# The first feed-forward's up projection as seven block products instead of eight

## The chip, the cores and the metric

The kernel runs on one core of a Trainium2 chip. Its time is the device time of that core in microseconds (us), from one launch; the time before is the median of three runs. The core has TensorE (PE; its weight loads are a row of their own, PEld), VectorE (DVE), ScalarE (ACT), GpSimd (POOL) and SyncE (SP), which issues most of the DMAs. Each engine works through its own queue of instructions in order; semaphores tie the queues together.

## The reference

A two-layer transformer on 512 latent tokens and 256 context tokens, model width 1024. Each layer has a mixer (attention in layer 0, a gated recurrence, HGRN2, in layer 1) and a feed-forward; before each of them comes a norm whose shift and scale come from conditioning vectors (the adaptive norm).

```python
def rms_norm(x, w):
    y = x * lax.rsqrt(jnp.mean(x * x, axis=-1, keepdims=True) + NORM_EPS)
    return y * w
def modulate(h, shift, scale):
    return h * (1.0 + scale) + shift
def swiglu(h, w_in, w_out):
    a, u = jnp.split(h @ w_in, 2, axis=-1)       # w_in is 1024 x 5632, a and u have 2816 columns
    return (jax.nn.silu(a) * u) @ w_out          # w_out is 2816 x 1024

for i in range(2):
    mod_l = silu(c) @ ada_w[i] + ada_b[i]        # 6 chunks of 1024; the same with c_ctx for the context
    ...
    h = h + gt1_l * y_l                          # the mixer
    h = h + gt2_l * swiglu(modulate(rms_norm(h, norm_ffn_w[i]), sh2_l, sc2_l), ffn_w_in[i], ffn_w_out[i])
    if not last:                                 # layer 0 alone: the context tokens too
        hc = hc + gt1_c * y_c
        hc = hc + gt2_c * swiglu(modulate(rms_norm(hc, norm_ffn_w[i]), sh2_c, sc2_c), ffn_w_in[i], ffn_w_out[i])
return rms_norm(h, final_norm_w)
```

So the first feed-forward runs on T = 768 tokens, the second on 512. In both, the hidden width 2816 is 22 tiles of 128, and the contraction over 1024 is 8 k-steps of 128.

## The kernel before

Activations lie transposed: the tile `hT[k]` holds 128 channels on its partitions and 768 tokens on its columns. Every fp32 product is made of three matmuls of a reduced format, in `mm3` (L104 to L107): each operand is split into a part hi, a cast on ACT (L82), and the rest lo, a subtraction on DVE or POOL (L85); then hi·hi (L105), hi·lo (L106) and lo·hi (L107) are summed in PSUM. Weights come through a ring: `load_split` loads a raw tile of 128 x 1024 floats (512 KB, four buffers) by a DMA on SP's queue and splits it into `whi` and `wlo` (three buffers each).

A feed-forward, `ffn`, goes over the hidden tiles in three parts of 8, 7 and 7 (`PARTS`). For each hidden tile, `chain` makes the gate half and then the up half: 8 k-steps, on the spans 0:512 and 512:770, three matmuls each. The spans hold the 768 tokens and two more columns, the shift of the two kinds of token, since the operands `fnh` and `fnl` (L780, L781) are the residual times the scale, without the norm and the shift. The norm's factor `rst`, one per token, is multiplied in behind the matmuls (`scaled`, L835 to L838), where the bias column is added too: silu on ACT (L861), the product on DVE (L865), and the split of the hidden tile into `gh` and `gl`. At the end of a part its 7 or 8 hidden tiles go through the down projection (`fo_chain`), whose result is added onto the residual (`residual`, L646).

The token factors come from `token_scale`: squares on ACT, their sums on DVE and POOL (L238), then `rstd_cols` (a matmul with ones, L245, a power on POOL, L250) and `rstd_psum` (a diagonal per 128 tokens on DVE, L258, times ones on PE, L259). They are made under the first two hidden tiles' matmuls. At the end of the first feed-forward, `norm_tail` does the same for layer 1.

The last output projection of attention (`wo_gen` with g = 3, PSUM tiles `wo` and `wos`) closes the attention's own filler queue, on the spans of 512 and 256 tokens.

Between hidden tiles and down-projection tiles, `fill.step` lets a side job take a few steps: the sums of the adaptive norm, `ada_acc`. Each step multiplies a 128 x 1024 piece of `ada_w` (`adw`) by a scalar and adds it (L220, L222), on DVE. In the first feed-forward it makes chunk 5 of layer 0, the gate of this feed-forward's own residual, and behind part 0 (`ada_last`) six chunks of layer 1. Chunk 4 of layer 0 is made on PE during attention (`ada_chunk`, 32-column matmuls, `pa`).

The program is written as one sequence; a scheduler puts each instruction in its engine's queue and sets semaphores, and pools of buffers set how far ahead a load may go.

Of the kernel before, what the change touches and what calls it, by code (L numbers as in the profile page):

```python
# [16 lines left out]
P = 128  # L17
# [13 lines left out]
PARTS = [(0, 8), (8, 7), (15, 7)]  # L31
# [12 lines left out]
def kernel(  # L44
# [11 lines left out]
    dma = nc.sync.dma_start  # L56

# [46 lines left out]
    def mm3(ps, ahi, alo, bhi, blo, first, last):  # L104
        PE.matmul(ps, ahi, bhi, start=first, stop=False)  # L105
        PE.matmul(ps, ahi, blo, start=False, stop=False)  # L106
        PE.matmul(ps, alo, bhi, start=False, stop=last)  # L107
# [85 lines left out]
    def ada_reduce(layer, ch, accs, load, fp):  # L193
        nv = len(accs)
        part = fp.tile([P, 2, 32], F32, tag="adpart", name=f"adpart{layer}{ch}")
        for v, a in enumerate(accs):
            turned = load(f"adt{layer}{ch}{v}")
            DVE.transpose(turned, a)
            DVE.tensor_reduce(part[:, v], turned.rearrange("p (j r) -> p j r", r=32), op=ALU.add, axis=AX.X)
            yield  # L200
        yield
# [9 lines left out]
    folds = []  # L211

    def ada_acc(layer, ch, accs, load, fp):
        for k in range(KT):
            raw = load(f"adw{layer}{ch}{k}")
            dma(raw, ada_w[layer, k * P : (k + 1) * P, ch * D : (ch + 1) * D])
            for v, a in enumerate(accs):
                cc = csil[:, v, k : k + 1]
                if k == 0:
                    DVE.tensor_scalar(a, raw, cc, None, op0=ALU.mult)  # L220
                else:
                    DVE.scalar_tensor_tensor(a, raw, cc, a, op0=ALU.mult, op1=ALU.add)  # L222
                yield
        yield from ada_reduce(layer, ch, accs, load, fp)

# [5 lines left out]
    def sumsq_add(acc, sqp, h, k, first, eng=None):  # L231
        if first:
            ACT.activation(acc, h, AF.Square)
        else:
            sq = sqp.tile([P, T], F32, tag="sq", bufs=2, name=f"sq{k}")
            sq = sq[:, : h.shape[1]]
            ACT.activation(sq, h, AF.Square)
            (eng or DVE).tensor_tensor(acc, acc, sq, op=ALU.add)  # L238

    def rstd_cols(pl, accs, n):  # L240
        nt = n // P
        pc = bank("ssq")
        for t in range(nt):
            for i, acc in enumerate(accs):
                PE.matmul(pc[:, 2 * t : 2 * t + 2], acc[:, t * P : (t + 1) * P], ones[:, 0:2],  # L245
                          start=(i == 0), stop=(i == len(accs) - 1))
# [1042 lines left out]
```

## Time and profile before

| what | us |
|---|---|
| runs (three) | 1898.82, 1902.82, 1902.89; median 1902.82 |
| profiled execution: its time | 1901.45 |
| profiled execution: span from first to last instruction | 1899.4 |
| front: projections, start of attention | 0 to 233 |
| attention | 233 to 438.95 |
| first feed-forward (768 tokens) | 438.95 to 1016.4 |
| HGRN2 | 1016.4 to 1510 |
| second feed-forward and output | 1510 to 1899.4 |

The bounds of the stages are those at which the first matmul of a stage's tiles starts. The mean granted clock of TensorE over the span was 0.988 of full speed. Rows of the page name a line of the code, an engine, an operation, the tile written, an arrow, the tiles read, the shape and the count; then the busy time, the mean duration of one in ns, and the idle time of the engine just before, with what released it. A row of the timeline starts with the start time and the duration, and ends, in brackets, with how long the engine had waited and for what. A matmul's duration there overlaps the next one's, since they are pipelined.

### The profile page before, as it was taken

The numbers are of one execution on the slowest core, as the hardware profiler recorded it, in microseconds if no ns is written. First come the engines' busy times: TensorE is split into PE (matmuls) and PEld (weight loads), VectorE is DVE, ScalarE is ACT, GpSimd is POOL, SyncE is SP. The second block draws the span as 40 slices with busy tenths as digits, with TensorE's granted clock in tenths as the row PEclk, the third lists the DMA queues.
The fourth block names the chain that finished last, engine by engine and source line by source line (L and its number), as shares of the span: only waits on it lengthen the run. The fifth ranks groups of instructions, "written<-read, shape, count | busy, mean of one in ns | idle before, by whom it ended". The sixth has DMA issues, their size and how long they took to land. (4 is left out here: it accounts for less than half of the span.)

```text
span 1899.4 us, 29674 instructions
## 1 busy us (share of the span) xinstructions
PE 1833.4 (97%) x12111; PEld 1633.3 (86%) x12111; DVE 1127.6 (59%) x1821; ACT 680.3 (36%) x1222; POOL 394.8 (21%) x401
## 2 busy tenths in 40 slices
PE   8989999998999999999998989999998999999998
PEld 6778788887888888888887979889897799898997
DVE  3676788888866446445545555564647744344444
ACT  3333877763321122112224423233333432222224
POOL 1243534532000000000002444354436100000000
PEclk9989999998999999999999999999999999999999
DMA  9433200012424235353321211111111133333331
GB/s 325 169 104 100 100 2 23 23 46 78 155 89 133 79 93 174 88 154 107 100 66 51 79 45 45 57 56 56 56 56 45 45 93 97 89 89 98 92 88 57
DMA packets 206152, 166.37 MB, mean 88 GB/s; under 512 B 6801, under 2 KB 189249, under 8 KB 206017
## 3 DMA queue, kind: packets, MB, share of 16 engines
q1 hardware_dynamic: 205728, 163.43, 28.1%
q8 instruction: 96, 1.57, 0.3%
q10 hardware_dynamic: 288, 1.05, 0.1%
q14 instruction: 40, 0.32, 0.1%
HBM read 162.36 MB, written 2.10 MB: 87 GB/s over the span
## 5 line engine op out<-in xcount | busy, mean ns | idle before, releaser
L106 PE MATMUL ffi<-fnl,whi_fi 128*128 128x258 f32 (+2 forms) x1408 | 439.5, 312 | 2.6 <-DVE fnl L781 2.6
L105 PE MATMUL ffi<-fnh,whi_fi 128*128 128x258 f32 (+2 forms) x1408 | 440.3, 313 | 1.4 <-ACT fnh L780 1.3
L107 PE MATMUL ffi<-fnh,wlo_fi 128*128 128x258 f32 (+2 forms) x1408 | 437.5, 311 | 0.0
L106 PEld LDWEIGHTS ffi<-fnl,whi_fi 128*128 128x128 f32 x1408 | 268.2, 190 | 19.3 <-DVE fnl L781 3.6
L105 PEld LDWEIGHTS ffi<-fnh,whi_fi 128*128 128x128 f32 x1408 | 266.8, 190 | 18.0 <-ACT fnh L780 1.5
L107 PEld LDWEIGHTS ffi<-fnh,wlo_fi 128*128 128x128 f32 x1408 | 267.2, 190 | 15.9
L82 ACT CAST whi_fi<-raw_fi 128x1024 fp32r<-128x1024 f32 x88 | 92.3, 1050 | 359.0 <-issue 190.3
L250 POOL TENSOR_TENSOR rc<-rc,mhalf 128x2 f32<-128x2 f32 (+2 forms) x6 | 6.4, 1068 | 929.0 <-DVE rc L248 929.0
L105 PE MATMUL ffo<-gh,whi_fo 128*128 128x512 f32 (+1 forms) x542 | 192.2, 355 | 0.9 <-DVE modc L206 0.5
L107 PE MATMUL ffo<-gh,wlo_fo 128*128 128x512 f32 (+1 forms) x542 | 190.8, 352 | 0.0
L106 PE MATMUL ffo<-gl,whi_fo 128*128 128x512 f32 (+1 forms) x542 | 190.7, 352 | 0.0
L646 DVE SCALAR_TENSOR_TENSOR hT<-ffo,modc,hT 128x512 f32<-128x512 f32 (+1 forms) x74 | 47.8, 648 | 128.7 <-PE ffo L107 128.6
L222 DVE SCALAR_TENSOR_TENSOR adacc<-adw,csil,adacc 128x1024 f32<-128x1024 f32 x70 | 88.3, 1280 | 57.5 <-DMA adw<-in_ada_w_dram 57.3
L82 ACT CAST whi_fo<-raw_fo 128x896 fp32r<-128x896 f32 (+1 forms) x48 | 47.0, 980 | 202.5 <-PE ffo L106 98.5
L105 PEld LDWEIGHTS ffo<-gh,whi_fo 128*128 128x128 f32 x542 | 101.9, 188 | 16.8 <-issue 1.5
L106 PEld LDWEIGHTS ffo<-gl,whi_fo 128*128 128x128 f32 x542 | 101.9, 188 | 15.4
L107 PEld LDWEIGHTS ffo<-gh,wlo_fo 128*128 128x128 f32 x542 | 101.8, 188 | 15.3
L1103 POOL TENSOR_TENSOR KD<-KD,tot 128x384 f32<-128x384 f32 x96 | 100.3, 1068 | 68.7 <-ACT kc L1086 67.1
L85 DVE TENSOR_TENSOR wlo_fi<-raw_fi,whi_fi 128x1024 fp32r<-128x1024 f32 x87 | 106.1, 1221 | 7.5 <-ACT whi_fi L82 6.5
L660 POOL TENSOR_SCALAR pf<-pf,st 128x768 f32<-128x768 f32 (+1 forms) x96 | 73.7, 769 | 119.3 <-DVE st L659 75.5
L85 DVE TENSOR_TENSOR ptl<-pt,pth 128x384 fp32r<-128x384 f32 (+1 forms) x160 | 79.5, 522 | 9.7 <-ACT pth L82 8.4
L1103 DVE TENSOR_TENSOR QD<-QD,tot 128x256 f32<-128x256 f32 x96 | 56.3, 626 | 42.2 <-PE lv L1096 42.0
(315 smaller groups left out, 4203.2 us busy)
## 6 DMA issues: line engine op xcount, KB each, us to landing
raw_fi<-in_ffn_w_in_dram SPq DMA_DIRECT2D x88, 512.0 KB, 3.8
adw<-in_ada_w_dram SPq DMA_DIRECT2D x80, 512.0 KB, 4.3
raw_fo<-in_ffn_w_out_dram SPq DMA_DIRECT2D x32, 448.0 KB, 3.6
raw_fo<-in_ffn_w_out_dram SPq DMA_DIRECT2D x16, 512.0 KB, 3.8
raw_hz<-in_hgrn_w_in_dram SPq DMA_DIRECT2D x14, 512.0 KB, 3.8
adr<-in_ada_w_dram SPq DMA_DIRECT2D x16, 256.0 KB, 4.5
adr<-in_ada_w_dram SPq DMA_DIRECT2D x8, 512.0 KB, 7.0
raw_wq<-in_attn_w_qkv_dram SPq DMA_DIRECT2D x8, 512.0 KB, 5.5
```

The costliest lines, as they stand in the source:

```text
L82: ACT.copy(hi, src)
L85: (eng or DVE).tensor_tensor(lo, src, hi.bitcast(F32), op=ALU.subtract)
L105: PE.matmul(ps, ahi, bhi, start=first, stop=False)
L106: PE.matmul(ps, ahi, blo, start=False, stop=False)
L107: PE.matmul(ps, alo, bhi, start=False, stop=last)
L222: DVE.scalar_tensor_tensor(a, raw, cc, a, op0=ALU.mult, op1=ALU.add)
L250: POOL.tensor_tensor(rc, rc, mhalf.to_broadcast([P, nt]), op=ALU.pow)
L646: DVE.scalar_tensor_tensor(hT[o][:, a:e], ps, mcol(layer, ch, o, v), hT[o][:, a:e], op0=ALU.mult, op1=ALU.add)
L660: POOL.tensor_scalar(pf, pf, st3[:, 2:3], 1.0, op0=ALU.mult, op1=ALU.mult)
L1103: eng.tensor_tensor(view, view, f, op=ALU.mult)
```

## The change

In the first feed-forward the up projection, seen as a product of a matrix of weight blocks and a matrix of activation blocks, two by two each, is made by Strassen's scheme, in seven block products instead of eight. For one pair (the gate and the up half of one hidden tile) the four weight blocks are a11 and a12 (gate, k-steps 0 to 3 and 4 to 7) and a21 and a22 (up, the same); the four activation blocks are b11, b12 (k-steps 0 to 3, first and second half of the 768 tokens) and b21, b22 (k-steps 4 to 7). Each block product is four k-steps of three matmuls with 384 columns. The products m1 to m7 of a pair run in the order m1, m5, m2, m6, m4, m3, m7. Their results are put together partly in PSUM, where m6 and m7 add onto m1's bank and m3 onto m5's, and partly by copies and subtractions in SBUF (c11, c12, c21, c22).

- **Weight sums.** Four of the seven products need a sum or a difference of weight blocks. They are made in the raw tile of the ring, by DMAs on POOL's queue that add to their destination (`gather`, L834): a21 += a22 when the tile is loaded (S1), a21 += a11 after the split for m5 (S2), then a11 += a21 as it lies in HBM (S3), and a21 += a12 after the split for m6 (S4). Splits are now 512 wide, two to a ring tile, and `split_ahead` keeps three ring tiles filled.
- **Activation sums.** They need the normalised operand, so `xhalf` makes x = norm(h) · scale + shift for one half of the tokens and splits it; t1 to t4 are differences of the blocks, made once, on POOL and DVE, and split.
- **Norm by token halves.** The sums of squares, `rstd_cols` and `rstd_psum` run once for each half of 384 tokens. `wo_last` makes the last output projection of attention by the same halves, inside the start of `ffn`. `rstd_psum` writes the whole diagonal in one DVE operation.
- **Two plain pairs first.** Hidden tiles 0 and 1 are made in the old way (eight k-steps on each of two halves of 384), while the differences are made.
- **Parts and fillers.** Five parts (5, 5, 4, 4, 4 hidden tiles). Chunk 5 of layer 0's adaptive norm moves to attention, on PE, beside chunk 4. `ada_acc` works in halves of 512 columns with a load two pieces ahead.
- The second feed-forward keeps the old code under the name `ffn_plain`.

The diff, cut to its core (`...` marks what is left out):

```diff
-PARTS = [(0, 8), (8, 7), (15, 7)]
+PARTS = [
+    [(0, 5), (5, 5), (10, 4), (14, 4), (18, 4)],
+    [(0, 8), (8, 7), (15, 7)],
+]
...
+    def ada_acc(layer, ch, nv, fp):
...
+        for hf in range(2):
+            accs = [fp.tile([P, 512], F32, tag=f"adacc{v}", name=f"adacc{layer}{ch}{hf}{v}") for v in range(nv)]
+            raws = [load(hf, 0), load(hf, 1)]
...
     def rstd_psum(dg, rc, n):
...
-            DVE.tensor_scalar(dg[:, sl], ident, rc[:, t : t + 1], None, op0=ALU.mult)
-            PE.matmul(pss[t // 4][:, (t % 4) * P : (t % 4 + 1) * P], ones, dg[:, sl], start=True, stop=True)
+        DVE.tensor_tensor(dg, ident.unsqueeze(1).to_broadcast([P, nt, P]), rc.unsqueeze(2).to_broadcast([P, nt, P]),
+                          op=ALU.mult)
...
+    HALVES = [[[(0, 0, 384)], [(0, 384, NL), (1, NL, T)]], [[(0, 0, 256)], [(0, 256, NL)]]]
...
-    pfill.add(ada_chunk(4, None, lambda: ap_.tile([P, T], F32, tag="pf", bufs=4, name="arows"), ring_raw))
+    for ch in (4, 5):
+        pfill.add(ada_chunk(ch, None, lambda: ap_.tile([P, T], F32, tag="pf", bufs=4, name="arows"), ring_raw))
...
+    def wo_last():
+        (ws, prs), = lasts
+        for half in HALVES[0]:
+            a0, e0 = half[0][1], half[-1][2]
+            for o in range(KT):
...
+    def ffn(layer, only_lat, pre, begin, tail=None):
...
+        def load_next():
...
+            if key[0] == "w" and key[1] >= 2 and key[2] == 1:
+                gather(raw[:, 0:512], raw[:, 512:1024])
+
+        def gather(dst, src):
+            POOL_dma(dst, src, accum_op=ALU.add)
...
+        for h in range(2):
+            hs = slice(h * H, (h + 1) * H)
+            for o in range(KT):
+                next(pre)
+                sumsq_add(acc_n[:, hs], fp, hT[o][:, hs], o, o == 0, DVE if o % 2 else POOL, tag="adraw", width=512)
+                if h == 1 and o == 1:
+                    rc[0] = rstd_cols(fp, acc_n[:, 0:H], H, "rc0")
+                if h == 1 and o == 3:
+                    rst[0] = rstd_psum(ctile("c22", 2), rc[0], H)
+                if h == 1 and o >= 5:
+                    xhalf(o - 5, 0)
...
+        for i in range(4):
+            b11, b12, b21, b22 = blocks(i)
+            POOL.tensor_tensor(b11, b11, b12, op=ALU.subtract)
+            xsplit("t1", i, b11)
...
+        def m1(j, g):
+            xy = s2("xy")
+            st = S[j] = dict(X=xy[:, 0:H], Y=xy[:, 512 : 512 + H])
+            prod(st["X"], g, "b11", True)
+            st["c11"] = ctile("c11", 2)
+            ACT.copy(st["c11"], st["X"])
...
+        def m6(j, g):
+            st = S[j]
+            prod(st["X"], g, "t2", False)
...
+        def m7(j, g):
+            st = S.pop(j)
+            prod(st["X"], g, "t3", False)
+            DVE.tensor_tensor(st["c22"], st["c22"], st["X"], op=ALU.subtract)
+            DVE.tensor_tensor(st["c21"], st["c21"], st["X"], op=ALU.subtract)
+            hidden_tiles(j)
+            for h, (a, b) in enumerate((("c11", "c21"), ("c12", "c22"))):
+                POOL.tensor_tensor(st[a], st[a], st[b], op=ALU.mult)
+                hs = slice(h * H, h * H + H)
+                split(gh[j][:, hs], gl[j][:, hs], st[a])
...
+            def s2_s3():
+                gather(a21(), a11())
+                gather(a11().rearrange("p (k n) -> p k n", n=P), pair_src(j, 1)[:, 0:4])
+
+            rows = [
+                (a11, m1, 1, None), (a21, m5, 1, s2_s3), (a12, m2, 0, None),
+                (a21, m6, 1, lambda: gather(a21(), a12())), (a22, m4, 1, None), (a21, m3, 0, None),
+                (a11, m7, 0, None),
+            ]
...
+        def split_ahead(i):
+            while nsplit[0] < len(units) and units[nsplit[0]]["at"] // 2 <= units[i]["at"] // 2 + 2:
+                split_next()
...
-    ffn(0, False, lambda fill, fp: fill.add(ada_ffn(0, 5, fp)), ada_last, tail=norm_tail)
+    ffn(0, False, wo_last(), ada_last, tail=norm_tail)
...
-    ffn(1, True, lambda fill, fp: None, lambda fill, fp: None, wo_pair(GH // 2 - 1))
+    ffn_plain(1, True, lambda fill, fp: None, lambda fill, fp: None, wo_pair(GH // 2 - 1))
```

How the change moves the instructions, at three places. First ACT's queue in the first feed-forward. Before, for two hidden tiles (`whi_fi_4_0` is the hi part of hidden tile 4's gate weights, `_1` of its up weights; `ta` is the gate, `tu` the product, `gh_2` its hi part):

```order
L82 CAST whi_fi_4_0_5948<-raw_fi_4_0_5947 128x1024
L82 CAST gh_2_5394<-tu 128x512
L82 CAST gh_2_5394<-tu 128x256
L82 CAST whi_fi_4_1_6019<-raw_fi_4_1_6018 128x1024
L861 ACTIVATE ta<-ta 128x512
L861 ACTIVATE ta<-ta 128x256
L82 CAST whi_fi_5_0_6074<-raw_fi_5_0_6073 128x1024
```

And now, from one pair's c11 to the next pair's, where `raw_('w', 7, 0)` is the raw tile of pair 7's gate weights (a11, a12), `raw_('w', 7, 1)` that of its up weights (a21, a22), and the `c` and `xy` of pairs 6 and 7 carry their own numbers:

```order
L87 CAST whi_w_6935<-raw_('w', 7, 0)_6731 128x512
L983 ACTIVATE c22_6917<-xy_6878 128x384
L87 CAST whi_w_6935<-raw_('w', 7, 1)_6771 128x512
L990 ACTIVATE c11_6891<-c11_6891 128x384
L996 COPY c12_6955<-xy_6878 128x384
L87 CAST whi_w_6973<-raw_('w', 7, 0)_6731 128x512
L1008 ACTIVATE c21_6971<-z_6958 128x384
L87 CAST whi_w_6973<-raw_('w', 7, 1)_6771 128x512
L1002 ACTIVATE c12_6955<-c12_6955 128x384
L87 CAST whi_w_7017<-raw_('w', 7, 1)_6771 128x512 x2
L87 CAST gh1_7009<-c12_6955 128x384
L977 COPY c11_7038<-xy_7025 128x384
```

Two casts of 1024 per pair have become seven of 512, and between them, in the same queue, stand the copies out of PSUM on which PE's next products wait; the casts from `raw_('w', 7, 1)` for m6 and m3 read a tile that a DMA has changed since the cast before.

Then POOL's queue. Before, in the first feed-forward, it has a few operations at the start and two powers at the end:

```order
L85 TENSOR_TENSOR wlo_fi_0_1_5487<-raw_fi_0_1_5485,whi_fi_0_1_5486 128x1024
L238 TENSOR_TENSOR acc_o<-acc_o,sq_5469 128x768
L238 TENSOR_TENSOR acc_o<-acc_o,sq_5475 128x768
L238 TENSOR_TENSOR acc_o<-acc_o,sq_5481 128x768
L250 TENSOR_TENSOR rc<-rc,mhalf 128x6
```

Now, through the whole stage, per pair (here pair 7, with S1 of pair 8 in between):

```order
L834 DMA raw_('w', 7, 1)_6771<-raw_('w', 7, 0)_6731 128x512
L834 DMA raw_('w', 8, 1)_6901<-raw_('w', 8, 1)_6901 128x512
L834 DMA raw_('w', 7, 0)_6731<-in_ffn_w_in_dram 128x4x128
L834 DMA raw_('w', 7, 1)_6771<-raw_('w', 7, 0)_6731 128x512
L1017 TENSOR_TENSOR c12_6955<-c12_6955,c22_6917 128x384
L1017 TENSOR_TENSOR c11_6891<-c11_6891,c21_6971 128x384
```

S2 of the pair stands first, S1 of the next pair behind it, then S3 and S4, and the two products of gate and up behind the four DMAs.

Last, PE's queue where attention ends and the feed-forward starts. Before, `wos` is the last output projection, and `fnh` the operand without the norm:

```order
L107 MATMUL wos<-qT_4919,wlo_wo_5205 128x256
L105 MATMUL ffi<-fnh,whi_fi_0_0_5409 128x512
L105 MATMUL ffi<-fnh,whi_fi_0_1_5486 128x512
L106 MATMUL ffi<-fnl,whi_fi_0_0_5409 128x512
L107 MATMUL ffi<-fnh,wlo_fi_0_0_5410 128x512
L105 MATMUL ffi<-fnh,whi_fi_0_0_5409 128x258
```

Now, where `xb11h` and `xb11l` are the hi and lo parts of the normalised first half, `w01h` the up weights of hidden tile 0, and `ssq` the sum of squares of the second half:

```order
L113 MATMUL wos<-o_4977,wlo_wo_5263 128x384
L111 MATMUL ffi<-xb11h,whi_w 128x384
L112 MATMUL ffi<-xb11l,whi_w 128x384
L113 MATMUL ffi<-xb11h,wlo_w 128x384
L111 MATMUL ffi<-xb11h,w01h 128x384
L112 MATMUL ffi<-xb11l,w01h 128x384
L258 MATMUL ssq<-ones,acc_n 128x2 x3
L113 MATMUL ffi<-xb11h,w01l 128x384
```

The feed-forward's first matmuls now read normalised operands, and those for the second half's norm stand among them.

More of the change, by code (lines that the diff above doesn't have):

```diff
@@ L209, in ada_reduce, with sumsq_add @@
         )
[L211 to L224, printed above, removed]
     def ring_raw(name):
         return ring.tile([P, 1024], F32, tag="raw", bufs=4, name=name)
-    def sumsq_add(acc, sqp, h, k, first, eng=None):
+    def sumsq_add(acc, sqp, h, k, first, eng=None, tag="sq", bufs=2, width=T):
         if first:
@@ L648 @@
     ap_ = pool("att", att)
+    o4es = ExitStack()
+    o4p = pool("o4p", o4es, side="right")
+    lasts = []
     def scores(h, t):
@@ L731, in third @@
                 prs = [ohs.pop(2 * g), ohs.pop(2 * g + 1)]
+                if g == KVH - 1:
+                    ws = [load_split(attn_w_o[0, k * P : (k + 1) * P, :], [P, D], f"wo{k}", POOL)
+                          for k in (2 * g, 2 * g + 1)]
+                    lasts.append((ws, prs))
+                    return
                 fill.add(wo_gen(g, [p_[0] for p_ in prs], [p_[1] for p_ in prs]))
@@ L933, in ada_ffn @@
         nv = 2 if layer == 0 or ch < 2 else 1
[L934 to L935 removed]
+        yield from ada_acc(layer, ch, nv, fp)
         if nv == 1:
```

376 lines of the change are left out of this document (336 added, 40 removed).

## The prediction

> **What bounds the kernel now.** I read the page's busy times first, then the same by stage, then the start times of single matmuls, and last what TensorE waited for in the stage that changes.
>
> ```profile
> PE 1833.4 (97%) x12111; PEld 1633.3 (86%) x12111; DVE 1127.6 (59%) x1821; ACT 680.3 (36%) x1222; POOL 394.8 (21%) x401
> ```
> ```profile
> 233.00:438.95 205.95, 199.08 (x1366) 178.70 (x1364) 174.41 (x392) 143.72 (x340) 83.20 (x92) 1.00 0.07 22
> 438.95:1016.40 577.45, 572.05 (x3248) 497.78 (x3248) 335.19 (x395) 137.60 (x197) 15.21 (x7) 0.99 0.37 110
> ```
>
> The second fence is the view by stage: length, then busy time of PE, PEld, DVE, ACT and POOL, granted clock, DMA share, GB/s. Attention runs from 233 to 438.95, the first feed-forward from there to 1016.4. In both PE is busy nearly all the time, so a matmul less there is time less. In the feed-forward DVE is busy 58% of the time, ACT 24% and POOL 3%: there is room beside PE, but on queues that run in order.
>
> Busy time of pipelined matmuls overlaps, so their price is read from start times, in the timeline at full clock:
>
> ```profile
> 446.78 0.39 PE L105 MATMUL ffi<-fnh,whi_fi 128*128 128x512 f32 x1
> 447.01 0.39 PE L106 MATMUL ffi<-fnl,whi_fi 128*128 128x512 f32 x1
> 447.24 0.40 PE L107 MATMUL ffi<-fnh,wlo_fi 128*128 128x512 f32 x1
> 447.47 0.29 PE L105 MATMUL ffi<-fnh,whi_fi 128*128 128x258 f32 x1
> ...
> 447.84 0.39 PE L105 MATMUL ffi<-fnh,whi_fi 128*128 128x512 f32 x1
> ```
>
> A 512-column matmul takes 0.23 us (446.78 to 447.47 for three), a 258-column one 0.123 (447.47 to 447.84 for three). A pair (gate and up of one hidden tile: 16 k-steps of three matmuls on each of two spans) costs 48 x 0.23 + 48 x 0.123 = 16.96 us, and 22 pairs 373 of the stage's 577 us. The rest is nearly all the down projection, whose matmul columns stay.
>
> **The matmuls.** 384 columns lie midway between 258 and 512; I take the mean, 0.177 us. No 384-column row exists; the ends are 0.123 and 0.23, and a linear cost is what two sizes suggest. A Strassen pair is 7 products x 4 k-steps x 3 = 84 matmuls, 14.8 us: 2.12 us less, x 20 pairs = **-42.4 us**. The two plain pairs keep 96 x 0.177 = 17.0: nothing. The last output projection of attention goes from 512+256 to 384+384 columns: nothing.
>
> **What the vector engines get per pair.** Durations of the nearest shapes, from the groups by form:
>
> ```profile
> L82 ACT CAST gh<-tu 128x512 fp32r<-128x512 f32 x44 | 27.3, 621 | 73.0 <-DVE tu L865 73.0
> L85 DVE TENSOR_TENSOR gl<-tu,gh 128x512 fp32r<-128x512 f32 x44 | 30.1, 685 | 5.8 <-ACT gh L82 5.8
> L85 DVE TENSOR_TENSOR gl<-tu,gh 128x256 fp32r<-128x256 f32 x22 | 9.2, 417 | 0.0
> L861 ACT ACTIVATE ta<-ta 128x512 f32<-128x512 f32 x44 | 31.7, 723 | 12.7 <-DVE ta L838 12.3
> L861 ACT ACTIVATE ta<-ta 128x256 f32<-128x256 f32 x22 | 10.9, 495 | 0.0
> L865 DVE SCALAR_TENSOR_TENSOR tu<-tu,ta 128x512 f32<-128x512 f32 x44 | 32.9, 748 | 2.3 <-ACT ta L861 0.6
> L1103 POOL TENSOR_TENSOR KD<-KD,tot 128x384 f32<-128x384 f32 x96 | 100.3, 1068 | 68.7 <-ACT kc L1086 67.1 <-DVE tot L1110 1.6
> ```
>
> ACT: 7 casts of 512 (0.62), 6 operations of 384 (0.5 to 0.6), 2 casts of 384 (0.5): 8.8 us of 14.8. DVE: 7 lo parts of 512 (0.69), 6 operations of 384 (0.55 to 0.6), 4 steps of the adaptive-norm sums (now 512 wide, 0.75): 4.8 + 3.4 + 3.0 = 11.2 us. POOL: two products of 384 (1.07) and four accumulating DMAs. Each fits beside PE by its sum alone, so I put these at nothing; if that cover goes, DVE is late first.
>
> **The gathers, the term I know least.** The seven products of a pair are split into hi and lo from the same two raw tiles, which are changed between the splits by DMAs that add. So the ACT queue holds, in order: cast m1, copy c22, cast m5 (and on DVE its lo part), then the sum S2, cast and lo of m6, then S4, cast of m3, a gh cast and the copy of c11, for which PE waits before m6. That is 3 x 0.62 + 0.6 + 0.69, then 0.62 + 0.69, then 0.5 + 0.55: 5.5 us, with 0.1 for some five hand-overs 6.0 us. It starts when PE frees the ring's oldest tile, and seven products, 14.8 us, lie between that and m6. So a pair lasts max(14.8, 6.0 + S2 + S4), each counted from the end of the DVE lo part to the landing. Behind the waiting ACT stand PSUM copies; behind the waiting POOL the gate products; and SP's next loads wait for the same splits. No DMA of before is issued by POOL or adds. The nearest rows:
>
> ```profile
> raw_fi<-in_ffn_w_in_dram SPq DMA_DIRECT2D x88, 512.0 KB, 3.8
> ...
> adr<-in_ada_w_dram SPq DMA_DIRECT2D x16, 256.0 KB, 4.5
> adr<-in_ada_w_dram SPq DMA_DIRECT2D x8, 512.0 KB, 7.0
> ...
> out_dram<-ob SPq DMA_DIRECT2D x2, 512.0 KB, 2.7
> ```
>
> From issue to landing they go from 2.7 to 7.0 us. At 2.7 each the pair is at 14.8 and nothing is lost (a gain is excluded: the products cannot be fewer). At 7.0 each it is 20.0, and 5.2 x 20 = 104 us are lost. A 256 KB sum reads 512 KB in all, so I take the 256 KB row, 4.5, for S2; S4 is issued some 1.5 us behind S3, which adds 512-byte runs from HBM on the same queue, so 5.0: 15.5, 0.7 us over, **+14 us**. The sum of the two has its turning point at 8.8 us, and at 10.5 the gain is gone.
>
> The Trainium skill, "DMA: Bandwidth & Descriptors", section "Anatomy of one DMA — SWDGE (gpsimd) path", gives about 2.0 us plus bytes over 436 GB/s for a DMA issued by POOL: an estimate of 2.6 us for 256 KB, which would make this term nothing and the forecast 1868. No run here shows such a DMA; for the 512 KB load from SP the same formula gives 3.2 where the trace has 3.8.
>
> **The start.** Before, the operands are scaled without the norm, and the token scale comes in after the matmuls, so PE starts early:
>
> ```profile
> 436.69 0.39 PE L105 MATMUL wos<-qT,whi_wo 128*128 128x256 f32 x1 [0.84 <-DVE hT L646]
> ...
> 438.95 0.90 PE L105 MATMUL ffi<-fnh,whi_fi 128*128 128x512 f32 x2 [1.28 <-ACT fnh L780]
> 441.32 0.79 PE L106 MATMUL ffi<-fnl,whi_fi 128*128 128x512 f32 x1 [1.46 <-DVE fnl L781]
> ```
> ```profile
> 435.00:440.00 5.00, 2.73 (x12) 1.44 (x10) 2.62 (x6) 2.77 (x5) 1.65 (x1) 0.93 0.00 0
> 440.00:445.00 5.00, 3.68 (x11) 3.11 (x12) 5.00 (x9) 5.00 (x11) 0.72 (x1) 0.50 0.36 105
> 445.00:450.00 5.00, 5.00 (x28) 4.38 (x28) 5.00 (x10) 4.54 (x7) 1.33 (x1) 0.88 0.00 0
> ```
>
> That costs 0.84 + 1.28 + 1.46 = 3.6 us idle and 5 x (0.07 + 0.50 + 0.12) = 3.5 us of clock: 7 us. In the change, the first half's norm runs under the second half's output projection. Then ACT must make the operands: 8 x (0.6 + 0.5) for the first half, 8 x (0.35 + 0.5 + 0.5) for the second in two spans, two casts of 1024 (2.1), three squares, a silu and a gh cast: 25 us. PE has some 2.5 + 17.0 us of its own there and 4.2 us that it takes ahead from pair 1, 24 us; and it stands in order behind the ssq matmuls of the second half, 2 to 4 us. To this comes POOL, which makes half the lo parts and eight differences, 17 or so operations of 1.07 us. In before the two engines hinder each other in this very place:
>
> ```profile
> 448.67 3.65 POOL L238 TENSOR_TENSOR acc_o<-acc_o,sq 128x768 f32<-128x768 f32 x1 [7.95 <-ACT sq L237]
> ```
> ```profile
> 449.00 0.74 DVE L220 TENSOR_SCALAR adacc<-adw,csil 128x1024 f32<-128x1024 f32 x1
> ...
> 450.53 2.34 DVE L220 TENSOR_SCALAR adacc<-adw,csil 128x1024 f32<-128x1024 f32 x1
> ```
>
> The same DVE operation takes 2.34 us instead of 0.74 until POOL is done. I add 5 us for that: 12 us lost against 7, **+5 us** (bounds -3 and +18: nothing lost but ACT's excess and the ssq wait; or all 17 POOL operations in series).
>
> The Trainium skill, "SBUF — State Buffer", section "Who interferes with whom", says that DVE with two SBUF inputs and a POOL operation that reads SBUF lock each other out for the whole instruction. The two rows agree in kind. By it the steady state too pays, for the two gate products.
>
> **The smaller terms.** Chunk 5 of the adaptive norm goes from DVE sums to 32 small matmuls in attention:
>
> ```profile
> L167 PE MATMUL pa<-adw,cpad 128*32 128x256 f32 x192 | 17.8, 409 | 0.0
> ```
>
> 17.8 / 192 x 32 = **+3 us**, on PE, which is full there. Its eight loads hide: attention's DMA share is 0.07. Five part ends instead of three: from the last product to gh it is two DVE subtractions, two POOL products, a cast and a lo part, 1.2 + 2.1 + 0.5 + 0.55 = 4.4 us, under some 3 to 4 us of other matmuls; with the thinner cover of four-tile chains (PSUM banks return after 1.4 us, not 2.5), **+3 us** (0 to +8). At the stage's end PE waits for the diagonal of the norm, twice:
>
> ```profile
> 1017.13 0.49 PE L259 MATMUL rstd<-dg,ones 128*128 128x128 f32 x2 [1.55 <-DVE dg L258]
> 1019.42 1.52 PE L259 MATMUL rstd<-dg,ones 128*128 128x128 f32 x6 [1.81 <-DVE dg L258]
> ```
>
> One operation now makes what six made, and the sums drained there are half as wide: **-2 us** (-3 to 0).
>
> Sum: -42.4 + 14 + 5 + 3 + 3 - 2 = -19.4. The profiled execution took 1901.45 us (span 1899.4), 1.4 below the median of the runs; I go from it to **1882 us**.
>
> **The rivals.**
>
> *The sums are hidden* (both land within 8.8 us together): the loads' 3.8 speaks for it, the shared DMA engines, 0.37 busy before and fuller now, against. -33.4: 1868 us.
>
> *The sums set the pace, slower than before.* One mechanism: ACT stands in cast m6 and again in cast m3 for a landing, c11 is copied late, PE waits at m6. It decides from 10.5 us for the two; at 6.2 each, near the 7.0 row, the pair takes 18.4, 3.6 x 20 = 72 us more: 1940 us.
>
> *DVE becomes the bound.* It has 11.2 us of work per pair, 13.3 if both POOL products lock it out. If the four gathers hold it too, 0.9 us each, it needs 17 us: 2.2 x 20 = 44 on 1868, 1912 us. Nothing in before shows a POOL DMA beside DVE, so this is open; below 0.4 us each it costs nothing.
>
> *The start costs its upper bound*: 13 us more than I say, 1895 us.
>
> **How the numbers follow.** Forecast 0.38, hidden sums 0.27, slow sums 0.14, DVE bound 0.12, start 0.09. Within 0.3% (5.7 us, about what a measurement here tells from no change) lie the start case in half and some of the DVE case: same 0.09; faster 0.38 + 0.27 + 0.04 = 0.69; slower 0.22. Four fifths lie between 1858, a little under the hidden case for the bounds of the small terms, and 1930, which leaves out most of the slow-sum case. Around the forecast alone I would say 1872 to 1895.
>
> **What would show it.** Start times 0.177 us apart for 384 columns; a matmul count of 84 per pair; starts of m1 in successive pairs 15.5 us apart (14.8, or over 17, by the rivals). In the waits, ACT casts of whi_w released by a DMA from POOL, and PE xy released by ACT c11, once per pair. POOL DMAs with 4 to 5 us to landing. DVE busy about three quarters of the feed-forward. Between the last output projection and pair 1, some 8 us of PE idle and a clock under 1.0. I am wrong if a sum takes over 5.3 us, if the lo parts take much over 0.69, or if the operands of the first pairs come later than counted.

## The result: 1976.44 us, 3.9% slower

| kernel | median us | against before (95% interval) |
|---|---|---|
| before | 1902.17 | |
| changed | 1976.44 | 1.0394 (1.0375 to 1.0414) |

The prediction was 1882 (1858 to 1930): the wrong sign, and outside the range. The profiled execution took 1977.19 us, its span is 1975.4. First the page of the changed kernel, with the queue that is new:

```profile
PE 1826.6 (92%) x11929; PEld 1654.1 (84%) x11929; DVE 1188.0 (60%) x2064; ACT 767.2 (39%) x1465; POOL 534.8 (27%) x541
...
q0 software_dynamic: 19200, 20.98, 6.9%
```

PE's share fell from 97% to 92%: there are fewer matmuls, and PE waits. Where, the first projection of HGRN2 behind the feed-forward tells (instructions of one tile, before and then after; the last two numbers are the first and the last start):

```profile
L105 PE MATMUL hv<-whi_hv,hnh x192: 279/283/366, 1051.4 to 1408.1; 128*128 128x256 f32 x192
```
```profile
L111 PE MATMUL hv<-whi_hv,hnh x192: 280/283/366, 1127.4 to 1484.1; 128*128 128x256 f32 x192
```

It starts 76.0 us later, as much as the span grew: nothing was lost or won behind this point. The stages of the changed kernel ahead of it (same columns as in the prediction): the start, the first three Strassen pairs, the rest, the end of the stage:

```profile
447.52:493.40 45.88, 38.74 (x205) 34.12 (x205) 44.17 (x77) 31.65 (x70) 23.66 (x22) 1.00 0.25 60
493.40:550.60 57.20, 46.66 (x242) 45.06 (x241) 40.77 (x66) 20.36 (x40) 11.30 (x11) 0.91 0.60 142
550.60:1078.50 527.90, 471.75 (x2538) 433.53 (x2536) 300.31 (x478) 162.52 (x310) 109.60 (x105) 0.95 0.54 131
1078.50:1095.40 16.90, 2.06 (x11) 1.80 (x9) 8.18 (x16) 3.37 (x6) 3.50 (x2) 0.64 0.38 120
```

And what PE waited for (total us, times, longest):

```profile
PE xy L111 <- ACT c L977: 49.3, 17, 5.8
PE ssq L258 <- DVE acc_n L252: 13.4, 2, 12.6
PE ffo L111 <- ACT gh L87: 8.2, 6, 1.9
PE xy L111 <- DVE c L1001: 4.6, 5, 1.5
PE ffo L111 <- DVE hT L660: 4.0, 6, 1.7
```

From the start times of all matmuls between attention's end and this projection I made a balance: each matmul's time to the next one's start, less its price at full clock (0.23 us for 512 columns, 0.1755 for 384, 0.1225 for 258, 0.12 for 256, in proportion to the columns for the few smaller ones). What is left over, idle time and slower clock together, is booked on the matmul that came late:

| us | before | after | difference |
|---|---|---|---|
| attention's end (last matmul of `po`) | 419.7 | 426.4 | +6.7 |
| left over from there to the end of the first two pairs | 15.5 | 15.7 | +0.2 |
| up projection at full clock | 372.2 | 328.5 | -43.7 |
| left over ahead of m5 | | 70.3 | +70.3 |
| left over ahead of the other products (before: in the other 20 pairs) | 2.2 | 15.3 | +13.1 |
| left over ahead of the down projection | 3.0 | 18.7 | +15.7 |
| left over behind it, up to the first projection of HGRN2 | 12.9 | 25.9 | +13.0 |

The differences make +75.3 of the 76.0 us. The gain came in full; four costs ate it: the waits ahead of the products, the down projection, the stage's end and the later start.

**The wait ahead of m5.** It comes once in each of most pairs. The timeline of PE at m5 of pairs 10, 11 and 12, then ACT's for the chain that ends at the second of them:

```profile
742.83 0.44 PE L111 MATMUL xy<-xt1h,whi_w 128*128 128x384 f32 x1 [1.82 <-ACT c L977]
762.62 0.69 PE L111 MATMUL xy<-xt1h,whi_w 128*128 128x384 f32 x1 [3.53 <-ACT c L977]
...
779.71 0.45 PE L111 MATMUL xy<-xt1h,whi_w 128*128 128x384 f32 x1 [1.08 <-ACT c L977]
```
```profile
748.65 0.62 ACT L87 CAST whi_w<-raw_('w', 11, 1)_7679 128x512 fp32r<-128x512 f32 x1 [0.30 <-PE xy L112]
...
755.59 0.62 ACT L87 CAST whi_w<-raw_('w', 11, 1)_7679 128x512 fp32r<-128x512 f32 x1 [2.14 <-DMA raw_('w', 11, 1)_7679<-raw_('w', 11, 0)_7637]
756.11 0.52 ACT L1002 ACTIVATE c<-c 128x384 f32<-128x384 f32 x1
760.75 0.62 ACT L87 CAST whi_w<-raw_('w', 11, 0)_7637 128x512 fp32r<-128x512 f32 x1 [4.12 <-DMA raw_('w', 11, 0)_7637<-in_ffn_w_in_dram]
761.28 0.92 ACT L87 CAST gh<-c 128x384 fp32r<-128x384 f32 x2
762.10 0.47 ACT L977 COPY c<-xy 128x384 f32<-128x384 f32 x1
...
778.25 0.62 ACT L87 CAST whi_w<-raw_('w', 12, 1)_7864 128x512 fp32r<-128x512 f32 x1 [1.18 <-DMA raw_('w', 12, 1)_7864<-raw_('w', 12, 0)_7822]
778.77 0.51 ACT L87 CAST gh<-c 128x384 fp32r<-128x384 f32 x1
779.19 0.47 ACT L977 COPY c<-xy 128x384 f32<-128x384 f32 x1
```
```profile
750.74 0.85 POOL L834 DMA_DIRECT2D raw_('w', 12, 1)_7864<-raw_('w', 12, 1)_7864  x1 [12.39 <-DMA raw_('w', 12, 1)_7864<-in_ffn_w_in_dram]
751.27 1.19 POOL L834 DMA_DIRECT2D raw_('w', 11, 1)_7679<-raw_('w', 11, 0)_7637  x1
755.85 1.30 POOL L834 DMA_DIRECT2D raw_('w', 11, 0)_7637<-in_ffn_w_in_dram  x1 [3.38 <-DMA raw_('w', 11, 1)_7679<-raw_('w', 11, 0)_7637]
```

At 748.65 ACT casts a21 for pair 11's m5, as soon as m6 of pair 10 has freed the place in the ring. POOL issues S2 at 751.27, behind S1 of pair 12, which had waited for its load. S2 has landed when m6's cast starts at 755.59; only then may S3 go (it overwrites the block that S2 reads), and it has landed when m7's cast starts at 760.75. ACT stands 4.12 us in the cast for m7, casts the two gh, and only then copies c11. PE takes up m5 0.05 us after that copy. From the end of m6 to m5, 14.0 us; PE has five products for it (m4, m3, m7, m1, m2), 10.5 us.

Pair 11 is one of the worse kind. In five pairs (3, 6, 11, 15, 19) S2 stands on POOL behind S1 of the next pair and is issued 1.2 to 1.8 us behind the lo part of m5; these are also the only five in which ACT waits for S3. In the other pairs S2 is issued 0.3 us behind that lo part, and ACT waits for S2 and then for S4, as at m3's cast of pair 12 above (778.25). Where no down projection lies between m6 and the next m5, in 15 pairs, the way from one to the other takes 13.3 us in the mean (9.9 to 16.7), and PE has four or five products for it, 9.6 us in the mean.

**The stage's end.** PE from the last down-projection matmul on, and DVE:

```profile
1078.40 0.28 PE L113 MATMUL ffo<-gh,wlo_w 128*128 128x256 f32 x1
1091.30 1.87 PE L258 MATMUL ssq<-ones,acc_n 128*128 128x2 f32 x8 [12.62 <-DVE acc_n L252]
```
```profile
1085.75 0.75 DVE L220 SCALAR_TENSOR_TENSOR adacc<-adw,csil,adacc 128x512 f32<-128x512 f32 x1 [1.73 <-DMA adw<-in_ada_w_dram]
1089.05 0.75 DVE L220 SCALAR_TENSOR_TENSOR adacc<-adw,csil,adacc 128x512 f32<-128x512 f32 x1 [2.55 <-DMA adw<-in_ada_w_dram]
1089.72 1.86 DVE L252 TENSOR_TENSOR acc_n<-acc_n,sq 128x512 f32<-128x512 f32 x3
```

The adaptive-norm sums were not done when the feed-forward was. DVE waits for one load after the other, 1.1 to 4.5 us from one piece to the next, and the last sums of squares, for which PE waits, are queued behind it. The loads, the squares and the diagonal share two buffers (`adraw`).

### The profile page after: what moved, and what is told of

It reads as the page before. It is cut to its first block, busy times and chain, and to the rows that moved or that the text cites. A ratio compares the mean times of both kernels' runs of the same rounds, so it can differ in the third digit from the quotient of the medians.

```text
span 1975.4 us, 30418 instructions
## 1 busy us (share of the span) xinstructions
PE 1826.6 (92%) x11929; PEld 1654.1 (84%) x11929; DVE 1188.0 (60%) x2064; ACT 767.2 (39%) x1465; POOL 534.8 (27%) x541
## 5 line engine op out<-in xcount | busy, mean ns | idle before, releaser
L112 PE MATMUL ffi<-fnl,whi_fi 128*128 128x256 f32 x704 | 198.0, 281 | 1.1 <-DVE fnl L1200 1.1
L111 PE MATMUL ffi<-fnh,whi_fi 128*128 128x256 f32 x704 | 198.8, 283 | 0.1
L113 PE MATMUL ffi<-fnh,wlo_fi 128*128 128x256 f32 x704 | 197.8, 281 | 0.0
L112 PEld LDWEIGHTS ffi<-fnl,whi_fi 128*128 128x128 f32 x704 | 133.2, 189 | 1.7 <-DVE fnl L1200 1.5
L111 PEld LDWEIGHTS ffi<-fnh,whi_fi 128*128 128x128 f32 x704 | 132.7, 189 | 0.4 <-issue 0.3
L113 PEld LDWEIGHTS ffi<-fnh,wlo_fi 128*128 128x128 f32 x704 | 132.8, 189 | 0.0
L111 PE MATMUL ffo<-gh,whi_w 128*128 128x512 f32 (+1 forms) x352 | 120.7, 344 | 12.3 <-ACT gh L87 8.2
L112 PE MATMUL ffo<-gl,whi_w 128*128 128x512 f32 (+1 forms) x352 | 119.3, 340 | 0.0
L113 PE MATMUL ffo<-gh,wlo_w 128*128 128x512 f32 (+1 forms) x352 | 119.2, 339 | 0.0
L220 DVE SCALAR_TENSOR_TENSOR adacc<-adw,csil,adacc 128x512 f32<-128x512 f32 x112 | 82.1, 754 | 46.2 <-DMA adw<-in_ada_w_dram 45.9
L111 PE MATMUL xy<-xt1h,whi_w 128*128 128x384 f32 x80 | 36.7, 459 | 49.4 <-ACT c L977 49.3
```

The source lines that it names most:

```text
L111: PE.matmul(ps, ahi, bhi, start=first, stop=False, **kw)
L112: PE.matmul(ps, ahi, blo, start=False, stop=False, **kw)
L113: PE.matmul(ps, alo, bhi, start=False, stop=last, **kw)
```

## The experiments

All changes are against the changed kernel, unless the kernel before is named. "Pair" is the mean time of one Strassen pair, from the start times of its products (379.9 / 20 in the changed kernel).

| run | median us | against before (95% interval) | pair us |
|---|---|---|---|
| changed | 1976.44 | 1.0394 (1.0375 to 1.0414) | 19.0 |
| sums by POOL's additions | 1936.89 | 1.0194 (1.0177 to 1.0211) | 16.6 |
| X and Y as two tiles | 1942.60 | 1.0222 (1.0205 to 1.0240) | 16.3 |
| no sums | 1913.71 | 1.0068 (1.0046 to 1.0090) | 15.6 |
| four shared buffers | 1958.96 | 1.0311 (1.0282 to 1.0339) | 18.7 |
| first, second and fourth together, three steps | 1918.00 | 1.0094 (1.0080 to 1.0108) | 16.1 |
| before, five parts | 1917.48 | 1.0089 (1.0076 to 1.0103) | |
| before, chunk 5 in attention | 1905.28 | 1.0026 (1.0016 to 1.0036) | |
| S3 alone by POOL | 1963.79 | 1.0332 (1.0318 to 1.0346) | 18.2 |
| c11's copy ahead | 1940.19 | 1.0204 (1.0187 to 1.0221) | 16.8 |
| that, two tiles, products on DVE | 1921.98 | 1.0105 (1.0088 to 1.0122) | 15.7 |
| that, four parts, three steps | 1925.77 | 1.0124 (1.0109 to 1.0139) | 16.9 |
| the last but one, four shared buffers | 1908.35 | 1.0041 (1.0027 to 1.0055) | 15.8 |

### Is it the sums?

```diff
-            POOL_dma(dst, src, accum_op=ALU.add)
+            POOL.tensor_tensor(dst, dst, src, op=ALU.add)
...
-                gather(a11().rearrange("p (k n) -> p k n", n=P), pair_src(j, 1)[:, 0:4])
+                POOL.tensor_tensor(a11(), a21(), a22(), op=ALU.subtract)
```

> The four weight sums per pair are made by POOL's own additions (S3 as a21 minus a22, from SBUF) instead of accumulating DMAs; all else as in the change. Theory A (PE waits at m5 because c11's copy stands in ACT's queue behind a cast that waits for a sum's landing): a sum takes 1.1 to 1.5 us instead of 4.4 to 4.9, successive m1 come 14.8 to 15.5 us apart instead of 19.3, the idle ahead of m5 falls from 50 us to under 10, and with the clock that comes back the kernel takes 1900 to 1920 us. Theory B (POOL's additions hold DVE, and DVE is the bound): pairs of 17 us or more, over 1935 us. If the sums are not the cause: 1970 us and more.

1936.89 us: 39.6 us less, but not the 1900 to 1920 of theory A; the time lies at the lower edge of theory B, the pair of 16.6 us a little under its 17. The waits of PE:

```profile
PE xy L111 <- ACT c L977: 16.6, 14, 3.0
...
PE xy L111 <- DVE c L1001: 9.9, 11, 2.4
```

Ahead of m5 33 us of idle went; the wait for DVE ahead of m7 doubled, from 4.6 us. In this run 28 of the 512-wide steps of the adaptive-norm sums run beside an operation of POOL and take 1.30 us in the median; the others take 0.75. The run of three edits below shows such a place.

The other way, without any sum:

```diff
-            POOL_dma(dst, src, accum_op=ALU.add)
+            pass
```

> The weight sums are left out altogether: all seven products read the weights as loaded, so the feed-forward's result is another one. This prices the sums from above. Theory A: pairs of 14.8 us, no idle ahead of m5, 1895 to 1910 us; what stays above the 1860 of the matmul count alone is the start, the part ends and the stage's end. Theory that the 384-column products or the vector engines' work set the pace: pairs stay over 17 us and the time over 1940.

1913.71 us, just above the range of theory A. So the sums cost 62.7 us, and the 384-column products do run as counted. But with sums that cost nothing the kernel is still 0.7% slower than before: the rest of the change, waits inside the pairs included, costs over 50 us. Part of the wait for c11 stays without any sum:

```profile
PE xy L111 <- ACT c L977: 8.2, 13, 1.1
```

The balance made for this run has 22 us lost ahead of all products, 12.5 of them ahead of m5.

### Is it the order, or the latency?

```diff
-            xy = s2("xy")
-            st = S[j] = dict(X=xy[:, 0:H], Y=xy[:, 512 : 512 + H])
+            st = S[j] = dict(X=xbank("xx")[:, 0:H], Y=xbank("xy")[:, 0:H])
```

(`xbank` gives a tile of one bank; the other users of two-bank tiles in this feed-forward take two of them.)

> The banks X and Y of a pair become two tiles of one bank each, so that m5, which writes Y, no longer waits for the copy of c11 out of X; the sums stay DMAs. Theory A with the wait at m5 put there by the shared tile: the loop from one m6 to the next loses m5's 2.1 us, pairs of about 17.2 us, 1930 to 1945 us. Rival (c11's copy isn't what m5 waits for, or the chain of S2 and S3 alone sets the pace): within 10 us of 1976.

1942.60 us, inside theory A's range: m5 now runs while ACT still waits, and the wait is m6's:

```profile
PE xx L114 <- ACT c L978: 20.9, 12, 4.0
```

That m5 waited for c11's copy at all was an effect of the shared tile, since it writes the other bank.

```diff
-            while nsplit[0] < len(units) and units[nsplit[0]]["at"] // 2 <= units[i]["at"] // 2 + 2:
+            while nsplit[0] < len(units) and units[nsplit[0]]["at"] // 2 <= units[i]["at"] // 2 + 1:
...
+            c11 = S.get(u.get("j"), {}).get("copy")
+            if c11 is not None and u["i"] in (5, 6,):
+                tc.add_manual_dep(cast.ins, c11.ins.name, mybir.DependencyInfo(mybir.DependencyClass.NoSync, mybir.DependencyReason.DATA), reason="order")
```

(5 and 6 are m3 and m7 in the list of a pair's products; the edge sets the order on ACT and waits for nothing.)

> The sums stay accumulating DMAs; only ACT's queue changes: c11's copy of a pair is ordered ahead of the casts of that pair's m3 and m7, which wait for S4 and S3 (and the splits run one ring tile ahead instead of two, so that this order is possible). If PE waits because the copy stands behind those casts: the idle ahead of m5 falls from 50 us to under 20, 1925 to 1945 us. If the latency of the sums sets the pace whatever the order (the casts then come late for their own products, and the wait moves to m3, m6 or m7): 1960 us and more.

1940.19 us, with the DMAs and their latency as they were. The wait line that answers to the 49.3 us:

```profile
PE xy L112 <- ACT c L978: 18.2, 11, 4.8
```

Two thirds of the idle time ahead of m5 were thus a matter of what stands before what in ACT's queue and of how far ahead the splits run; the run does not separate the two.

The third sum alone, the other three staying DMAs:

```diff
-                gather(a11().rearrange("p (k n) -> p k n", n=P), pair_src(j, 1)[:, 0:4])
+                POOL.tensor_tensor(a11(), a21(), a22(), op=ALU.subtract)
```

> Only the third sum, S3, is made by POOL from SBUF (a21 minus a22); S1, S2 and S4 stay accumulating DMAs. If the chain is S2, then S3 (which must wait until S2 has read a11), then m7's cast and c11's copy behind it: some 3.5 us per pair go, pairs of about 16 us, 1925 to 1945 us. If the chain is S2 and S4, as the prediction counted it: S4 is issued some 4 us earlier at most, and m3's cast still waits for it: 1955 us and more.

1963.79 us: 12.7 us less only, on the side of S2 and S4. Of the time that ACT's weight casts stood waiting for sums in the changed kernel (the rows of its waits added up), 73.5 us were for S2 and S4 and 20.7 for S3, five casts; here 63.0 for S2 and S4 and 1.6 for the S3 that POOL makes. The S3 that I had read out of pair 11 blocks the copy in five pairs only; in the others S2 and S4 do.

### The other costs, one at a time

```diff
-            raw = fp.tile([P, 512], F32, tag="adraw", bufs=2, ...)
+            raw = fp.tile([P, 512], F32, tag="adraw", bufs=4, ...)
...
-            raws = [load(hf, 0), load(hf, 1)]
+            raws = [load(hf, k) for k in range(4)]
```

> The adaptive-norm sums, the squares and the diagonal share four buffers of 128 x 512 instead of two, and loads run four pieces ahead instead of two. If the 12.6 us idle of PE at the stage's end come from sums that wait one load's latency for every two pieces: that idle falls under 3 us and the kernel takes 1962 to 1968 us. If the waits come from crowded DMA engines (share 0.54 in the stage): within 4 us of 1976.

1958.96 us, 17.5 us less, a little more than expected: at the stage's end the 12.6 us became 1.8, and the pairs gained 0.3 us each, 6 us in all.

```profile
PE ssq L258 <- DVE acc_n L252: 2.3, 2, 1.8
```

```diff
-PARTS = [(0, 8), (8, 7), (15, 7)]
+PARTS = [(0, 5), (5, 5), (10, 4), (14, 4), (18, 4)]
+PARTS1 = [(0, 8), (8, 7), (15, 7)]
...
-        for part, (j0, nj) in enumerate(PARTS):
+        parts = PARTS if layer == 0 else PARTS1
+        for part, (j0, nj) in enumerate(parts):
```

> The kernel before with five parts (5, 5, 4, 4, 4) in the first feed-forward and nothing else. My forecast put two more part ends at 3 us (0 to 8): 1901 to 1909 us. If the thinner cover by four-tile chains is what costs the 17 us that PE waits ahead of the down projection in the changed kernel, it shows here too: 1911 us and more. If those come from the longer chain behind m7 (subtractions, POOL products, cast, lo part), this kernel stays within 5 us of before.

1917.48 us: five parts cost 17.7 us in the kernel before, without Strassen, sums or POOL products. PE's waits:

```profile
PE ffo L106 <- DVE hT L647: 6.3, 11, 1.1
...
PE ffo L106 <- ACT gh L83: 3.7, 2, 3.0
```

The first line is the thinner cover that the prediction had in its +3: with shorter chains the residual on DVE comes too late to free the PSUM banks, eleven times. All idle time ahead of the down projection makes 10.9 us (0.9 in the kernel before), the lost time 19.8 (3.0): the gaps cost more than their length. In the window of the second part's down projection the clock is 0.91 (in the kernel before it is 1.00 from 587 to 640 us, at its first).

```profile
672.00:708.00 36.00, 34.54 (x176) 29.32 (x177) 21.09 (x27) 5.54 (x8) 0.00 (x0) 0.91 0.45 140
```

The last edit alone in the kernel before:

```diff
-    pfill.add(ada_chunk(4, None, ...))
+    for ch in (4, 5):
+        pfill.add(ada_chunk(ch, None, ...))
...
-    ffn(0, False, lambda fill, fp: fill.add(ada_ffn(0, 5, fp)), ada_last, tail=norm_tail)
+    ffn(0, False, lambda fill, fp: None, ada_last, tail=norm_tail)
```

> The kernel before with chunk 5 of the adaptive norm made on PE during attention and nothing else. Forecast: 3 us for its 32 matmuls, 1904 us. The changed kernel's attention ends 6.7 us later than before: if all of it is this chunk, 1906 to 1909 us, less what DVE gives back in the feed-forward's start (0 to 3 us).

1905.28 us, 5.5 us more, between the two.

### Together

The engine sums, the two tiles and the four buffers, and with them:

```diff
-                                  pe=lambda g, o=o: fo(p_, o, g), steps=2, done=("fo", p_, o)))
+                                  pe=lambda g, o=o: fo(p_, o, g), steps=3, done=("fo", p_, o)))
```

> The three edits together: sums by POOL's additions, two tiles for X and Y, four buffers with loads four pieces ahead for the adaptive-norm sums (and three of their steps per down-projection tile instead of two). If the three costs are separate: from the 1937 of the engine sums alone, the 22 us ahead of m5 mostly go and 13 to 18 us at the stage's end: 1893 to 1910 us. If the waits only move (to m6, which needs c11's copy in any case, and to the gh casts ahead of the down projection): 1915 us and more.

1918.00 us, on the side of "the waits only move". DVE's and POOL's timelines of this run at one place:

```profile
645.47 4.71 DVE L223 SCALAR_TENSOR_TENSOR adacc<-adw,csil,adacc 128x512 f32<-128x512 f32 x3 [0.78 <-DMA adw<-in_ada_w_dram]
```
```profile
644.93 1.29 POOL L837 TENSOR_TENSOR raw_('w', 9, 1)_7100<-raw_('w', 9, 1)_7100 128x512 f32<-128x512 f32 x1 [8.56 <-DMA raw_('w', 9, 1)_7100<-in_ffn_w_in_dram]
646.18 1.75 POOL L837 TENSOR_TENSOR raw_('w', 8, 1)_6937<-raw_('w', 8, 1)_6937,raw_('w', 8, 0)_6933 128x512 f32<-128x512 f32 x1
648.00 1.62 POOL L1092 TENSOR_TENSOR raw_('w', 8, 0)_6933<-raw_('w', 8, 1)_6937 128x512 f32<-128x512 f32 x1
```

Three DVE operations of 0.75 us take 4.71 us while POOL adds beside them. The latency was exchanged for DVE time; c11's copy now stands in most pairs behind gh casts that wait for POOL's products (61.5 us in all).

So I tried to keep the DMAs and order the work around them: the two tiles, the order with m6 in the list too, and

```diff
-                POOL.tensor_tensor(st[a], st[a], st[b], op=ALU.mult)
+                DVE.tensor_tensor(st[a], st[a], st[b], op=ALU.mult)
```

> The order of ACT's queue as in the run before, for m6's cast too where it can be, with X and Y as two tiles, and the two products of gate and up on DVE instead of POOL, where they stand behind two waits for sums. The sums are still DMAs. If the latency can be hidden by order alone: against the two tiles alone (1943 us) the 21 us idle ahead of m6 and some 10 us ahead of the first down projection go, 1908 to 1922 us. If DVE is too full for the two products (0.55 us each, 22 us in all): 1930 us and more.

1921.98 us, pairs of 15.7: with the latency of the sums untouched, the pair is 1.0 us from the matmul count (84 x 0.1755 = 14.7). What is left, by the same balance, is 20 us in the pairs, 13 of them ahead of m3, whose cast waits for S4, and 21 us ahead of the down projection; the wait at the stage's end is as long as in the change.

```profile
PE xy L115 <- ACT whi_w L90: 5.2, 4, 2.6
```

```diff
-    [(0, 5), (5, 5), (10, 4), (14, 4), (18, 4)],
+    [(0, 6), (6, 6), (12, 5), (17, 5)],
...
-                                  pe=lambda g, o=o: fo(p_, o, g), steps=2, done=("fo", p_, o)))
+                                  pe=lambda g, o=o: fo(p_, o, g), steps=3, done=("fo", p_, o)))
```

> As the run before, with four parts (6, 6, 5, 5) instead of five and three steps of the adaptive-norm sums per down-projection tile instead of two. The kernel before with five parts was 17.7 us slower than with three, so one part less should give some 9 us; the sums that drain at the stage's end should be done there, 10 to 13 us: 20 us under the run before, 1888 to 1902 us. If the steps only crowd DVE earlier: under 10 us gained.

1925.77 us: no gain. The end of the stage got better (its 11.9 us went), and the products' waits came back:

```profile
PE xx L115 <- ACT whi_w L90: 12.5, 5, 5.4
```

DVE stood 72.5 us for loads of the adaptive norm instead of 58.2. At the longest of these five waits (5.4 us, pair 9) it stood for them in the midst of the pair; the products of gate and up behind them on DVE came late, and m6's cast stood on ACT behind the gh casts that waited for those products. Whether the fourth part gained its 9 us can't be told from this run.

Last, back to five parts and two steps, with the four shared buffers as the only addition to the run of 1921.98 us:

```diff
-            raw = fp.tile([P, 512], F32, tag="adraw", bufs=2, name=f"adw{layer}{ch}{hf}{k}")
+            raw = fp.tile([P, 512], F32, tag="adraw", bufs=4, name=f"adw{layer}{ch}{hf}{k}")
...
-            raws = [load(hf, 0), load(hf, 1)]
+            raws = [load(hf, k) for k in range(4)]
```

> The run with order, two tiles and products on DVE (1922 us), with the four shared buffers and loads four pieces ahead of the second kind of edit; five parts and two steps as in the change. If the waits of the stage's end are a cost of their own, as in the run where they alone were taken away (17 us): 1902 to 1908 us, level with before or a little above. If, as with three steps per tile, DVE's queue then only waits for loads elsewhere: 1915 us and more.

1908.35 us, just above the 1902 to 1908 that were expected: 13.6 us less than without the four buffers. It is the best version found, 68 us faster than the change and still 0.4% slower than before. No version beat the kernel before.

## Why the prediction was wrong

**The matmuls: right.** -42.4 forecast, -43.7 in the balance. A 384-column matmul starts 0.174 us after the one before, in the median of the run (0.177 assumed). For instance:

```profile
445.75 0.34 PE L113 MATMUL wos<-o,wlo_wo 128*128 128x384 f32 x1
445.93 0.34 PE L111 MATMUL wos<-o,whi_wo 128*128 128x384 f32 x1
446.11 0.34 PE L112 MATMUL wos<-o,whi_wo 128*128 128x384 f32 x1
```

**The gathers: +14 forecast, +70 ahead of m5 and +83 ahead of all products measured, 63 of it gone without the sums. This is the step that failed.** Its sizes were good. A sum takes, by the DMA issues (pairs 18 and 15 are the ends of the 20 rows for S2 and S4; then an S1, then an S3):

```profile
raw_('w', 15, 1)_8496<-raw_('w', 15, 0)_8492 POOLq DMA_DIRECT2D x2, 256.0 KB, 6.2
...
raw_('w', 18, 1)_9334<-raw_('w', 18, 0)_9330 POOLq DMA_DIRECT2D x2, 256.0 KB, 3.6
...
raw_('w', 8, 1)_6901<-raw_('w', 8, 1)_6901 POOLq DMA_DIRECT2D x1, 256.0 KB, 4.2
...
raw_('w', 10, 0)_7550<-in_ffn_w_in_dram POOLq DMA_DIRECT2D x1, 256.0 KB, 4.4
```

I had 4.5 and 5.0, and a chain of 15.5 us; from m6 to the next m5 it is 14.0 in pair 11 and 13.3 in the mean. The path was right in most pairs too: S2, then S4, then c11's copy. What was wrong is its cover: "seven products, 14.8 us, lie between that and m6". The trace has four or five, 10.5 us in pair 11: the chain starts when m6 of the pair before has freed its place, not earlier, and ends at m5, not at m6, because X and Y are one tile and m2 has been moved ahead of m5. 14.0 - 10.5 is the 3.5 us that PE waits at pair 11; with the slower clock that follows, the left-over time ahead of m5 is 70.3 / 20 = 3.5 us per pair, where I had 0.7. With two tiles the chain ends at m6, m5 is cover too, and the left-over time ahead of m6 is 29 / 20 = 1.5 us per pair. The two runs that give cover back, by the tile and by the order, show it without touching a sum: 34 and 36 us, 54 for both with the products on DVE.

The rival that I put at 0.14 ("the sums set the pace") has the mechanism, ACT standing in casts with the copy behind it, but a wrong condition: I made it depend on slower sums, over 10.5 us for the two, and it came with the sums that I had expected.

By the formula of the Trainium skill, "DMA: Bandwidth & Descriptors", section "Anatomy of one DMA — SWDGE (gpsimd) path", I had an estimate of 2.6 us; the rows, of DMAs that add, have 3.6 to 6.2. By that page the term would have been nothing; the measurement decides.

**DVE as the bound: no.** The rival needed POOL's DMAs to hold DVE for 0.9 us each. The 512-wide sums take 0.75 us beside them, as alone; DVE is busy 300 of 528 us, not three quarters. It came true another way, in the runs where POOL adds.

**The start: +5 forecast, +0.2 measured** (from attention's end to the end of the first two pairs). PE waited eleven times, 0.2 to 1.2 us each, nearly always for an operand, and the clock stayed at 1.00 there, where I expected under 1.0; most of the part of POOL that I had put in series was hidden.

**Part ends: +3 (0 to 8) forecast, +15.7 in the balance, 17.7 alone in the kernel before.** The term had the right parts, the chain from m7 to gh at two more ends and the PSUM banks that come back late from the residual in a four-tile chain, but was far too small. The banks alone make eleven waits, 6.3 us, in the kernel before with five parts, and the slower clock behind such gaps had no place in the term.

**The stage's end: -2 (-3 to 0) forecast, +13.0 measured; with the cause removed the kernel gained 17.5 us, 6 of them in the pairs.** The diagonal did gain, 0.9 us. I looked at the diagonal and not at what stands ahead of it on DVE: halved pieces double the number of loads, with two buffers, and squares in the same two.

**Chunk 5: +3 forecast, +6.7 in the trace, +5.5 alone.** Only the matmuls were counted; what the rest is made of is not shown.

With the measured values, the sum is that of the balance: +75.3.

## What to carry to other kernels

A latency counts against the work that lies between the place where its chain can start and the instruction that is queued behind its end, so count the products between these two in the order of the queues; tiles that are shared for convenience and in-order queues move both places. A change that saves work on the engine that bounds the kernel must be charged with what makes room for it: here smaller parts, shared buffers and moved side jobs cost some 40 us, nearly as much as the products that were saved. Before sums are moved from one engine to another, look at what the two do to each other when they run side by side.

## What the runs showed of the hardware

- An accumulating DMA issued by POOL, 256 KB, takes 3.3 to 6.4 us to land in the changed kernel (80 of them, median 4.5) and shows on POOL for 0.85 to 1.3 us; the four per pair did not slow DVE, whose 512-wide steps take 0.75 us beside them and without them.
- POOL's additions on SBUF do: DVE's 0.75 us became 4.71 / 3 = 1.57 us. The Trainium skill, "SBUF — State Buffer", section "Who interferes with whom", says that a DVE instruction with two SBUF inputs contends with a GpSimd instruction that reads SBUF; the rows agree, with both engines slowed (POOL's 1.29 us became 1.75). The DVE rows that the prediction set beside this rule (L220) have one tensor and a scalar per partition as input, so they did not bear on it.
- Short gaps in PE cost more than their length. Ahead of m5 there are 49.3 us of idle time and 70.3 us of lost time; the granted clock was 0.91 and 0.95 in the two stretches of Strassen pairs, 0.99 in the same stage of the kernel before.
